# The embedding's products for four output tiles moved ahead, and the last gate product run as three tiles and one

## The chip, the core and the metric

The kernel runs on one core of one Trainium2 chip. The time is that of one execution on the device, in microseconds (us); "before" is the median of three runs. The engines are TensorE (PE, matmuls, with its weight loads as PEld), VectorE (DVE), ScalarE (ACT), GpSimd (POOL), and SyncE (SP), which here only issues DMA transfers.

## The reference, cut to what matters

One layer of a hybrid encoder block on 512 tokens of width 2048: two mixers, their gated merge, an output projection added to the residual, then a gated projection of the per-layer embedding `p` (256 wide), and a final RMSNorm:

```
merged = sigmoid(ga) * (a_out @ w_a_out) + sigmoid(gb) * (b_out @ w_b_out)
r = x + merged @ w_o
y = r + (p @ w_ple) * sigmoid(r @ w_ple_gate)
out = rmsnorm(y, final_gain)
```

## The kernel before, in words

Activations lie transposed, 128 channels by 512 tokens to a tile; 2048 channels are 16 tiles. Every product is made of float32 operands split in two parts of reduced type, high and low: high times high, high times low, low times high, that is three matmuls. ACT copies a tile to its high part and DVE subtracts it for the low part (line 136 and 141 for weights, 740 and 741 for activations, in `split`). Big products go in pairs of tiles through `gemm_pair` (line 264), seven products of half size each.

The order of every engine's instructions is the order in which the Python program emits them. `step()` is called after every third matmul or so; it runs functions that `later(n, f)` has put off by n steps, and takes one from the list `todo`. `split_to` and `load_to` split and load weights ahead of use (three and eight blocks ahead). Loads are issued by SP, in order.

SBUF tiles come from pools. `U(...)` gives one of `U_BUFS = 70` slots of 128x512 float32, `B(...)` one of 5 larger ones, raw weights one of 7. A tile holds its slot from the first instruction that touches it to the last one. Where no slot is free, the instruction that first writes the new tile waits for the last reader of a tile that gives one up, and its engine, in order, with it.

Towards the end of the program come these stages.

- `project_b`, 16 tiles of the second mixer's output projection, with the attention heads in between (ps_w, L196 to L198), then the first mixer's projection and the merge.
- the output projection in eight `gemm_pair` calls; in the last one `p_load` (L1165 to 1168) loads each half of the embedding from `pT` and splits it 22 steps later, and the parts of r that don't stay in SBUF are loaded again.
- the loop over 12 tiles of `p @ w_ple` (L1209 to 1230): six matmuls of 512 columns each into ps_pw, and ACT copies the result to a tile `pw`.
- six `gemm_pair` calls for 12 tiles of the gate, with `finish_y` behind them.
- the last four tiles (channels 1536 to 2047), in two pieces. For the first 384 tokens (slice `A`) `wide` (L1315 to 1335) goes over the 16 chunks k of r; for every k it makes three matmuls of 384 columns for each of the four tiles (ps_pg). Then ACT takes the sigmoid of all four; for each tile 6 matmuls give the embedding's product (ps_pw, L1332 to 1334), and DVE, POOL and ACT multiply, add to r, square, sum into `acc` and scale (L1346 to 1352). For the last 128 tokens (`C3`) `wide` is called again with tokens as rows ("natural"): 16 times three matmuls of 512 columns into ps_tg, then six for the embedding (ps_tw). Six steps into it `a_rms` has PE sum `acc` (ps_ms, L414), four steps later PE broadcasts the root (ps_bc, L425), and `a_out` scales and stores the 16 tiles (L1364).

While the natural piece runs, these U tiles are still to be read by it or behind it: 16 high and 16 low parts of r (`rh`, `rl`), the parts of ten weight blocks of 512 columns (20 tiles `wh4`, `wl4`: eight of the gate, two of the embedding), four parts of the embedding, `rn`, `fgn`, and 8 finished tiles (`pw`, of the first eight outputs). Before the natural piece, the four tiles `sg` of the gate's sigmoids are live as well.

Of the kernel before, what the change touches and what calls it, by code (L numbers as in the profile page):

```python
# [9 lines left out]
F32 = mybir.dt.float32  # L10
F32R = mybir.dt.float32r
# [23 lines left out]
def block_kernel(tc, xT, pT, posb, posq, w_in, w_v, w_ik, w_a, w_b, w_o, w_ple, w_gate,  # L35
# [4 lines left out]
    with contextlib.ExitStack() as ctx:  # L40
# [306 lines left out]
        u_p = [block(w_ple[:, 8 * q:8 * q + 8], (8,)) for q in range(MF // 4)]  # L347
# [759 lines left out]

        def project_b(m):
            gate_load(m + 2)
            pw = gemm(u_wb[m], bparts, "ps_w")  # L1110
            s = gates.popleft()
            dve.tensor_mul(s, pw, s)
            later(4, lambda: sp.dma_start(mbs[m], s))

        for m in range(16):
            project_b(m)
# [48 lines left out]
        def p_load(k):  # L1165
            t = U("pk")
            sp.dma_start(t, pT[:, k, :])
            later(22, lambda: pparts.append(split(t, "p", 1)))
# [40 lines left out]
        for m in range(MF):  # L1209
# [5 lines left out]
            ps = P("ps_pw")  # L1215
            for k in range(2):
                a, b = pparts[k]
                w = 2 * (m % 4) + k
                pe.matmul(ps, h[:, w], a, start=(k == 0), stop=False)
                pe.matmul(ps, h[:, w], b, start=False, stop=False)  # L1220
                pe.matmul(ps, l[:, w], a, start=False, stop=(k == 1))
                step()
# [6 lines left out]
            act.activation(t, ps, AF.Copy)  # L1229
            pws.append(t)  # L1230
# [4 lines left out]


        A, C3 = slice(0, 384), slice(384, 512)
# [98 lines left out]

        pgs = [P("ps_pg") for _ in range(4)]
        wide(u_t[0], rparts, pgs, range(4), False)
        sg = [U("sg") for _ in range(4)]
        for j in range(4):  # L1340
            act.activation(sg[j][:, A], pgs[j][:, A], AF.Sigmoid)
        for j in range(4):
            pw = P("ps_pw")
            wide(u_t[1], pparts, [pw], [j], False)
            y = ys[MF + j]
            dve.tensor_mul(sg[j][:, A], pw[:, A], sg[j][:, A])  # L1346
            (pool if j % 2 else dve).tensor_add(y[:, A], y[:, A], sg[j][:, A])
            act.activation(sg[j][:, A], y[:, A], AF.Square)
        for j in range(4):
            dve.tensor_add(acc[0][:, A], acc[0][:, A], sg[j][:, A])  # L1350
            y = ys[MF + j]
            act.activation(y[:, A], y[:, A], AF.Copy, scale=fg[:, MF + j:MF + j + 1])
# [177 lines left out]
```

## Time and profile before

| | |
|---|---|
| median of 3 runs | 1676.93 us (1675.07 to 1679.52) |
| the profiled execution | 1676.27 us, its span 1674.5 us |
| mean granted TensorE clock | 0.998 of full speed |
| PE busy | 1656.5 us, 99% |
| DVE, ACT, POOL busy | 1360.5, 927.8, 266.8 us |
| DMA | mean 228 GB/s, 381 MB |

The span goes from the first to the last instruction of the program; 1.8 us lie outside it. Busy matmuls overlap each other, so that the distance between starts is the cost of one. The rows of the trace stand below.

### The profile page before, as it was taken

How to read it: one execution, taken by the hardware profiler on the slowest of the kernel's cores; microseconds unless marked ns; L12 is line 12 of the kernel's file. 1: busy time of each engine (PE TensorE's matmuls, PEld its weight loads, DVE VectorE, ACT ScalarE, POOL GpSimd, SP SyncE). 2: the span in 40 equal slices, each digit the busy share in tenths (PEclk: the TensorE clock that was granted, in tenths of full speed). 3: DMA queues.
4: the chain of work that ended last, by engine and by line, in shares of the span. 5: the costliest groups of instructions: out<-in, count | busy, mean ns of one | idle time of the engine just before them, and what ended most of it. 6: DMA issues, size and time to landing. Idle time of an engine off the chain costs nothing.

```text
span 1674.5 us, 25823 instructions
## 1 busy us (share of the span) xinstructions
PE 1656.5 (99%) x9400; PEld 1446.7 (86%) x9400; DVE 1360.5 (81%) x2195; ACT 927.8 (55%) x1414; POOL 266.8 (16%) x266
## 2 busy tenths in 40 slices
PE   9999999999999999999999999999999999999997
PEld 7988888888888888888888888888888888888896
DVE  7898698988888888888888778676668888898895
ACT  7465455555555555455555545566643455477673
POOL 3100011111111111111331111100000243301202
PEclk9999999999999999999999999999999999999999
DMA  7536889788788788788998878999866699998873
GB/s 290 180 115 226 242 223 241 165 225 218 167 233 214 190 219 221 172 205 221 259 234 217 237 213 224 248 335 354 278 201 196 170 264 284 276 334 240 214 238 120
DMA packets 144608, 381.09 MB, mean 228 GB/s; under 512 B 15841, under 2 KB 32097, under 8 KB 144481
## 3 DMA queue, kind: packets, MB, share of 16 engines
q1 hardware_dynamic: 108416, 264.08, 45.8%
q0 software_dynamic: 26848, 98.58, 32.2%
q10 hardware_dynamic: 9216, 16.78, 2.8%
q8 instruction: 74, 1.21, 0.3%
q14 instruction: 54, 0.43, 0.1%
HBM read 326.82 MB, written 52.56 MB: 227 GB/s over the span
## 4 chain that ended last, share of the span: by engine, by line
PE 39%; DMA 8%; DVE 6%; ACT 2%; issue 1%; POOL 0%; SPq 0%; DVEq 0%; ACTq 0%
PE ps_p L264 13%; PE ps_v L264 8%; PE ps_r L264 4%; PE ps_q L264 4%; PE ps_w L196 2%; PE ps_w L197 2%; PE ps_w L198 2%; DVE wl L141 2%; DMA wraw<-w_o 1%; DMA mbs<-sg 1%; DMA sg<-sgb 1%; DVE e_t L234 1%; DMA wraw<-w_in 1%; ACT wh L136 1%; DMA bm<-scr 1%
## 5 line engine op out<-in xcount | busy, mean ns | idle before, releaser
L141 DVE TENSOR_TENSOR wl<-wraw,wh 128x1024 fp32r<-128x1024 f32 (+2 forms) x489 | 590.2, 1212 | 160.0 <-ACT wh L136 155.1
L136 ACT ACTIVATE wh<-wraw 128x1024 fp32r<-128x1024 f32 (+2 forms) x489 | 504.7, 1043 | 261.5 <-DVE wraw L143 125.3
L104 POOL DMA_DIRECT2D wraw<-w_in x132 | 116.8, 946 | 838.7 <-DVE wl L141 274.0
L230 ACT ACTIVATE e<-ps_p 128x512 f32<-128x512 f32 x174 | 103.8, 597 | 147.1 <-PE ps_p L264 138.0
L264 PE MATMUL ps_p<-hs,wh 128*128 128x512 f32 x704 | 177.0, 393 | 0.0
L264 PEld LDWEIGHTS ps_p<-hs,wh 128*128 128x128 f32 x704 | 126.5, 189 | 22.7
L264 PE MATMUL ps_p<-hs,wl 128*128 128x256 f32 x704 | 99.5, 283 | 0.8 <-DVE wl L141 0.8
L264 PEld LDWEIGHTS ps_p<-hs,wl 128*128 128x128 f32 x704 | 90.7, 191 | 2.1 <-DVE wl L141 1.2
L264 PE MATMUL ps_r<-hs,wh 128*128 128x512 f32 x352 | 90.4, 395 | 0.3 <-ACT wh L136 0.3
L264 PE MATMUL ps_p<-ha,wh 128*128 128x512 f32 x352 | 88.4, 392 | 0.0
L264 PE MATMUL ps_v<-ha,wh 128*128 128x512 f32 x352 | 88.2, 392 | 0.0
L264 PE MATMUL ps_q<-ha,wh 128*128 128x512 f32 x352 | 88.1, 392 | 0.0
L264 PE MATMUL ps_v<-hs,wh 128*128 128x512 f32 x352 | 86.9, 389 | 0.0
L915 DVE TENSOR_TENSOR go<-e_t 128x256 f32<-128x256 f32 x176 | 74.8, 425 | 6.2
L264 PEld LDWEIGHTS ps_v<-hs,wh 128*128 128x128 f32 x352 | 66.1, 188 | 13.8
L264 PEld LDWEIGHTS ps_v<-ha,wh 128*128 128x128 f32 x352 | 65.4, 188 | 13.5 <-issue 0.2
L264 PEld LDWEIGHTS ps_p<-ha,wh 128*128 128x128 f32 x352 | 63.2, 189 | 11.5 <-issue 0.3
L264 PEld LDWEIGHTS ps_q<-ha,wh 128*128 128x128 f32 x352 | 63.3, 189 | 11.3
L143 DVE TENSOR_TENSOR wraw<-wraw 128x1024 f32<-128x1024 f32 x58 | 71.0, 1225 | 2.0
L264 PEld LDWEIGHTS ps_r<-hs,wh 128*128 128x128 f32 x352 | 62.7, 189 | 11.3 <-ACT wh L136 0.5
L234 DVE TENSOR_TENSOR e_t<-ps_p,pv 128x512 f32<-128x512 f32 x52 | 35.8, 689 | 37.9 <-ACT e L230 37.8
L924 ACT ACTIVATE go<-go 128x512 f32<-128x512 f32 x40 | 25.3, 633 | 53.7 <-DVE go L915 53.7
(413 smaller groups left out, 3595.5 us busy)
## 6 DMA issues: line engine op xcount, KB each, us to landing
wraw<-w_in SPq DMA_DIRECT2D x190, 512.0 KB, 5.7
wraw<-w_in POOLq DMA_DIRECT2D x132, 512.0 KB, 8.4
wraw<-w_o SPq DMA_DIRECT2D x32, 512.0 KB, 8.1
wraw<-w_o POOLq DMA_DIRECT2D x24, 512.0 KB, 8.9
wraw<-w_gate SPq DMA_DIRECT2D x24, 512.0 KB, 5.4
wraw<-w_gate POOLq DMA_DIRECT2D x18, 512.0 KB, 6.6
wraw<-w_v SPq DMA_DIRECT2D x16, 512.0 KB, 4.6
wraw<-w_b SPq DMA_DIRECT2D x16, 512.0 KB, 6.9
```

Source lines behind the costliest of these rows:

```text
L104: pool.dma_start(out=raw_tiles[r], in_=src[:, k0:k0 + 8, :], accum_op=OP.add)
L136: act.activation(h, raw, AF.Copy)
L141: dve.tensor_sub(l, raw, h.bitcast(F32))
L143: dve.tensor_add(raw, raw, view(raw_tiles[plus], nk, cols))
L196: pe.matmul(o, h[:, k, w], a, start=(s == order[0]), stop=False)
L197: pe.matmul(o, h[:, k, w], b, start=False, stop=False)
L198: pe.matmul(o, l[:, k, w], a, start=False, stop=(s == order[-1]))
L230: act.activation(E[n], src, AF.Copy)
L234: f(t, x, y)
L264: pe.matmul(o[:, c], w[:, k], X[PRODUCTS[n]][k][:, c], start=(n < 4 and part == 0 and k == order[0]), stop=(part == parts[1] and k == orde ...
L915: dve.tensor_add(o[:, q], c0, c1)
L924: act.activation(o, o, func)
```

## The change

Four things are changed.

1. The embedding's halves are loaded and split once, in `project_b` before m = 9 and m = 12, stored as four tiles in DRAM (`ps_d`), and `p_load` loads the ready parts from there, both times it is called.
2. The loop of ps_pw goes over 16 tiles, the last four with 384 columns; a fourth block of `w_ple` is loaded and split for it. Their results are stored to DRAM (`pw_d`) and loaded again into four tiles `pw4` eight steps into the last gate stage.
3. In that stage `wide` is called for three tiles and then for the fourth; behind each call stand the sigmoid, product, sum, square and scaling of those tiles (`gated`). The 24 matmuls of ps_pw there are gone.
4. All sums of these tiles with r go to DVE; two of four were POOL's.

```diff
-        u_p = [block(w_ple[:, 8 * q:8 * q + 8], (8,)) for q in range(MF // 4)]
+        u_p = [block(w_ple[:, 8 * q:8 * q + 8], (8,)) for q in range(4)]
...
+        ps_d, pw_d = dp.tile([4, 128, L], F32, name="ps_d"), dp.tile([4, 128, L], F32, name="pw_d")
+
+        def p_split(k):
+            t = U("pk")
+            sp.dma_start(t, pT[:, k, :])
+
+            def both():
+                for i, part in enumerate(split(t, "p", 1)):
+                    later(8 + i, lambda i=i, part=part: sp.dma_start(ps_d[2 * k + i], part.bitcast(F32)))
+
+            later(12, both)
...
         for m in range(16):
+            if m in (9, 12):
+                p_split(m // 12)
             project_b(m)
...
         def p_load(k):
-            t = U("pk")
-            sp.dma_start(t, pT[:, k, :])
-            later(22, lambda: pparts.append(split(t, "p", 1)))
+            parts = U("ph", F32R), U("pl", F32R)
+            for i in range(2):
+                sp.dma_start(parts[i].bitcast(F32), ps_d[2 * k + i])
+            pparts.append(parts)
...
-        for m in range(MF):
+        A, C3 = slice(0, 384), slice(384, 512)
+        for m in range(16):
...
+            c = ALL if m < MF else A
             for k in range(2):
-                a, b = pparts[k]
+                a, b = pparts[k][0][:, c], pparts[k][1][:, c]
                 w = 2 * (m % 4) + k
-                pe.matmul(ps, h[:, w], a, start=(k == 0), stop=False)
+                pe.matmul(ps[:, c], h[:, w], a, start=(k == 0), stop=False)
...
-            act.activation(t, ps, AF.Copy)
-            pws.append(t)
+            act.activation(t[:, c], ps[:, c], AF.Copy)
+            if m < MF:
+                pws.append(t)
+            else:
+                later(6, lambda t=t, m=m: sp.dma_start(pw_d[m - MF, :, A], t[:, A]))
...
+        pw4 = [U("pw") for _ in range(4)]
+
+        def pw_loads():
+            for j in range(4):
+                sp.dma_start(pw4[j][:, A], pw_d[j, :, A])
+
+        later(8, pw_loads)
         pgs = [P("ps_pg") for _ in range(4)]
-        wide(u_t[0], rparts, pgs, range(4), False)
         sg = [U("sg") for _ in range(4)]
-        for j in range(4):
-            act.activation(sg[j][:, A], pgs[j][:, A], AF.Sigmoid)
-        for j in range(4):
-            pw = P("ps_pw")
-            wide(u_t[1], pparts, [pw], [j], False)
-            y = ys[MF + j]
-            dve.tensor_mul(sg[j][:, A], pw[:, A], sg[j][:, A])
-            (pool if j % 2 else dve).tensor_add(y[:, A], y[:, A], sg[j][:, A])
-            act.activation(sg[j][:, A], y[:, A], AF.Square)
-        for j in range(4):
-            dve.tensor_add(acc[0][:, A], acc[0][:, A], sg[j][:, A])
-            y = ys[MF + j]
-            act.activation(y[:, A], y[:, A], AF.Copy, scale=fg[:, MF + j:MF + j + 1])
+
+        def gated(js):
+            for j in js:
+                act.activation(sg[j][:, A], pgs[j][:, A], AF.Sigmoid)
+            for j in js:
+                y = ys[MF + j]
+                dve.tensor_mul(sg[j][:, A], pw4[j][:, A], sg[j][:, A])
+                dve.tensor_add(y[:, A], y[:, A], sg[j][:, A])
+                act.activation(sg[j][:, A], y[:, A], AF.Square)
+            for j in js:
+                dve.tensor_add(acc[0][:, A], acc[0][:, A], sg[j][:, A])
+                y = ys[MF + j]
+                act.activation(y[:, A], y[:, A], AF.Copy, scale=fg[:, MF + j:MF + j + 1])
+
+        for js in (range(3), range(3, 4)):
+            wide(u_t[0], rparts, [pgs[j] for j in js], js, False)
+            gated(js)
```

## Rows read from the trace of the kernel before

**Rows 1.** The page: busy us, share of the span, instructions.

```profile
PE 1656.5 (99%) x9400; PEld 1446.7 (86%) x9400; DVE 1360.5 (81%) x2195; ACT 927.8 (55%) x1414; POOL 266.8 (16%) x266
```

**Rows 2.** PE's waits over the span: us in total, times, longest.

```profile
PE ps_b L1395 <- POOL rl L1391: 3.7, 1, 3.7
...
PE ps_p L264 <- ACT wh L136: 1.6, 2, 1.3
...
PE ps_p L264 <- ACT e L230: 0.8, 1, 0.8
...
PE ps_mb L1303 <- DVE acc L1299: 0.2, 1, 0.2
```

**Rows 3.** Busy time by stretch: PE, PEld, DVE, ACT, POOL, clock, DMA share, GB/s.

```profile
1100.00:1200.00 100.00, 100.00 (x512) 85.48 (x511) 65.58 (x146) 65.34 (x143) 6.97 (x8) 1.00 1.01 337
...
1450.00:1500.00 50.00, 47.88 (x251) 40.99 (x250) 42.25 (x78) 33.30 (x66) 9.12 (x9) 1.00 1.01 319
...
1600.00:1625.00 25.00, 25.00 (x147) 23.68 (x146) 24.66 (x34) 17.43 (x28) 1.29 (x1) 1.00 0.69 238
```

**Rows 4.** PE in order of time, the last stages: start us, us.

```profile
1476.03 0.39 PE L1219 MATMUL ps_pw<-ph,wh 128*128 128x512 f32 x1
...
1496.58 2.11 PE L264 MATMUL ps_p<-ra,wh 128*128 128x512 f32 x8 [1.31 <-ACT wh L136]
...
1611.41 0.33 PE L1332 MATMUL ps_pg<-rh,wh 128*128 128x384 f32 x1
...
1645.87 0.33 PE L1332 MATMUL ps_pw<-ph,wh 128*128 128x384 f32 x1
...
1650.03 0.39 PE L1328 MATMUL ps_tg<-wh,rh 128*128 128x512 f32 x1
...
1654.16 0.72 PE L414 MATMUL ps_ms<-ones,acc 128*128 128x1 f32 x6
...
1663.52 0.39 PE L1330 MATMUL ps_tw<-wh,pl 128*128 128x512 f32 x1
```

**Rows 5.** ACT in order of time, around the loop of ps_pw.

```profile
1468.68 0.62 ACT L740 ACTIVATE ph<-pk 128x512 fp32r<-128x512 f32 x1
...
1495.47 1.06 ACT L136 ACTIVATE wh<-wraw 128x1024 fp32r<-128x1024 f32 x1
1496.41 1.09 ACT L1229 ACTIVATE y<-ps_pw 128x512 f32<-128x512 f32 x2
```

**Rows 6.** DVE in order of time, the last gate stage and behind it.

```profile
1618.40 1.22 DVE L141 TENSOR_TENSOR wl<-wraw,wh 128x1024 fp32r<-128x1024 f32 x1
...
1647.18 0.56 DVE L1346 TENSOR_TENSOR sg<-ps_pw,sg 128x384 f32<-128x384 f32 x1 [7.46 <-PE ps_pw L1334]
1647.77 0.56 DVE L1347 TENSOR_TENSOR y<-y,sg 128x384 f32<-128x384 f32 x1
1648.25 0.55 DVE L1346 TENSOR_TENSOR sg<-ps_pw,sg 128x384 f32<-128x384 f32 x1
...
1650.80 3.17 DVE L1350 TENSOR_TENSOR acc<-acc,sg 128x384 f32<-128x384 f32 x4
...
1664.10 0.41 DVE L1384 TENSOR_TENSOR sg<-ps_tw,sg 128x256 f32<-128x256 f32 x1
```

**Rows 7.** ACT in order of time, the last gate stage.

```profile
1644.57 1.99 ACT L1341 ACTIVATE sg<-ps_pg 128x384 f32<-128x384 f32 x4 [5.57 <-PE ps_pg L1334]
1648.37 0.53 ACT L1348 ACTIVATE sg<-y 128x384 f32<-128x384 f32 x1 [1.80 <-DVE y L1347]
...
1652.69 2.12 ACT L1352 ACTIVATE y<-y,g_sb 128x384 f32<-128x384 f32 x4
```

**Rows 8.** SP's waits from 1590 to 1640 us.

```profile
SPq L1268 <- DVE y L1245: 4.1, 1, 4.1
```

**Rows 9.** The stretches around PE's last idle time (columns as in rows 3).

```profile
1667.00:1668.00 1.00, 0.43 (x3) 0.43 (x4) 0.10 (x1) 0.45 (x1) 0.51 (x1) 1.00 1.03 361
1668.00:1669.00 1.00, 0.28 (x3) 0.09 (x1) 0.69 (x4) 0.44 (x2) 0.49 (x2) 0.77 1.04 372
1669.00:1670.00 1.00, 0.00 (x0) 0.00 (x0) 1.00 (x6) 0.00 (x0) 0.80 (x2) 0.50 1.03 352
```

**Rows 10.** PE's first matmuls of the program.

```profile
1.26 4.45 PE L401 MATMUL ps_warm<-warm 128*128 128x512 bf16 x10 [1.26 <-DVE warm L396]
```

More of the change, by code (lines that the diff above doesn't have):

```diff
@@ L1215, in block_kernel @@
             ps = P("ps_pw")
+            c = ALL if m < MF else A
             for k in range(2):
-                a, b = pparts[k]
+                a, b = pparts[k][0][:, c], pparts[k][1][:, c]
                 w = 2 * (m % 4) + k
-                pe.matmul(ps, h[:, w], a, start=(k == 0), stop=False)
-                pe.matmul(ps, h[:, w], b, start=False, stop=False)
-                pe.matmul(ps, l[:, w], a, start=False, stop=(k == 1))
+                pe.matmul(ps[:, c], h[:, w], a, start=(k == 0), stop=False)
+                pe.matmul(ps[:, c], h[:, w], b, start=False, stop=False)
+                pe.matmul(ps[:, c], l[:, w], a, start=False, stop=(k == 1))
                 step()
@@ L1228, in block_kernel @@
                 t = ypair[m // 2][:, L * (m % 2):L * (m % 2) + L]
-            act.activation(t, ps, AF.Copy)
-            pws.append(t)
+            act.activation(t[:, c], ps[:, c], AF.Copy)
[3 more added lines that the diff above has]
+                later(6, lambda t=t, m=m: sp.dma_start(pw_d[m - MF, :, A], t[:, A]))
         ys = {}
-        A, C3 = slice(0, 384), slice(384, 512)
         def finish_y(m, s, r):
```

## The prediction

> **What bounds the kernel now.** I read the page first: PE is busy 99% of the span [rows 1]. So a change wins only where PE waits or in the end behind PE's last matmul, and a matmul that is moved costs the same elsewhere. PE's waits are few [rows 2]. The longest, 3.7 us, lies in the end; of the others 0.8 us (on ACT's copy of `e`) and 1.3 of the 1.6 us (on ACT's `wh`) frame the loop that the change lengthens. The stretch from 1450 to 1500 us shows those two as 2.12 us of PE idle, at a DMA share of 1.01 [rows 3]. The order of time gives the last stages [rows 4]: the gate stage starts at 1611.41, its 24 matmuls of ps_pw take 1645.87 to 1650.03 (4.16 us, 0.173 each), the natural piece starts at 1650.03, PE sums `acc` at 1654.16, and its last matmul starts at 1663.52. In between PE never pauses, but DVE is nearly as full in the gate stage, 24.66 of 25 us [rows 3]. The end hangs on two things that finish together: PE's ps_tw, and DVE's scaling of the tiles, behind which the tail's first product starts at 1664.10 [rows 6].
>
> **Part 1, the matmuls.** The 24 leave the gate stage and come into the ps_pw loop, with as many columns: 4.16 us less, 4.16 us more, 0 in sum.
>
> **Part 2, around the loop.** ACT and DVE lose the embedding's splits there (two of 0.62 us on ACT [rows 5]), which now lie in `project_b`, where PE waits for nothing at 66% DVE and 65% ACT [rows 3]; there they cost nothing, and if that cover is gone, their 1.2 us. ACT's copy of `e`, 0.81 us late, comes 1.2 us earlier, so that pause should vanish. PE's pause of 1.31 us at 1496.58 [rows 4] comes from a `wh` that starts at 1495.47 behind queued copies of ps_pw [rows 5]. In the new loop PE needs it 4.2 us later, while ACT in front of it gets one more block of `w_ple` (1.06) and the four copies that came after it (2 x 1.1), 3.3 us, less the 1.2 for the splits. So most of this pause goes as well. I take -1.5 us for both. Bounds: -2.1 (both gone) and +1.5. The upper bound is for DMA: this stretch gains 512 KB of weights, 512 KB in `p_load`, and 768 KB of stores, 1.8 MB, 5.6 us at its 319 GB/s [rows 3], against 4.2 us of PE time. The 1.5 MB more in `project_b` come near 1173 and 1196 us, beside a busy DMA (share 1.01) but loads that are eight blocks ahead: I take 0.
>
> **Part 3, three tiles and one.** With four tiles PE spends 12 matmuls on a chunk k, 2.08 us; with three, 9, 1.56 us. It eats weights and parts of r by a third faster, and DVE, full, makes them in the same order as before. Chunk 4 needs a low part that is ready at 1618.40 + 1.22 = 1619.62 [rows 6], 8.2 us behind the start of the stage. Before, PE wanted it 8.33 + 0.35 = 8.7 us behind the start; now at 6.24 + 0.35 = 6.6. That is a wait of 1.7 us on DVE, which was none. From there DVE's order shifts in favour of the weights, and the remaining chunks keep pace within half a microsecond by my count, with SP's queue (four loads of `pw4` and four parts of the embedding instead of two halves, in front of the later gate weights) the most doubtful. I take +2.2; bounds 0 (DVE starts the stage earlier) and +4 (loads late).
>
> **Part 4, the slots.** The price here is not a duration but a count. A new tile waits for a slot's last reader: in the trace SP waits 4.1 us for DVE's L1245 before a load into a tile of the B pool, whose slot the last gate tile gives up there [rows 8]. In the U pool, at the end of the three tiles' pass, live are 8 `pw`, 32 parts of r, 20 parts of weights, 4 of the embedding, `rn` and `fgn`: 66. Before, the four `sg` made it 70, exactly the pool. Now `pw4` holds four from early in the stage, so 70 are taken before any `sg`. The first U tile to be freed is the high part of r's first tile, after the second matmul of the natural piece. So the sigmoids that should run under the fourth tile's pass wait until that pass is over. Nothing on PE waits for them until `acc` is summed; on ACT everything queues behind the first sigmoid.
>
> Counted from the start of the natural piece (T): the second matmul is through at 0.63 (starts 0.23 apart: 18 matmuls in 4.13 us [rows 4]). ACT starts 0.1 us later; sigmoids follow at 0.48 (four in 1.99 [rows 7]). DVE does product and sum at 0.59 and 0.48 from start to start [rows 6], on DVE alone since POOL is dropped: product 0 at 1.29, sum 2 over at 4.58, squares by 5.15 (0.53 each), third `acc` sum over at 6.24. Behind the squares ACT's queue holds three scalings (0.53 each [rows 7]) to 6.7, then the fourth sigmoid to 7.2; product, sum, square and `acc` of tile 3 add 2.3: about 9.55, and PE starts its sum at 9.7. Before it did at 4.13 (`acc` was ready at 1650.80 + 3.17 = 1653.97, just in time [rows 6]). PE therefore stands 5.6 us inside the natural piece, with ten steps of it and all of `a_out` behind. Those keep their distances, so the end moves by 5.6. Bounds: 0 (a slot is free after all) and 6.5.
>
> **Part 5, the clock.** After PE's last long matmul (over at 1663.91) the granted clock is still 1.00 in 1667 to 1668, falls in the next microsecond (0.77), and is 0.50, 1.2 GHz, after it [rows 9]: some 4.6 us, with only small matmuls in between. A pause of 5.4 us is longer, so I let the clock fall. For the way back the nearest row is the start: ten matmuls of 512 columns take 4.45 us [rows 10], 0.445 each against 0.229 later, though the profile's clock column there shows no fall. Half speed over 4.5 us costs 2.2. Bounds 0 and 4.
>
> The Trainium skill (TensorE: Matmul & The Clock Gate, part 1 on the clock gate) says that the throttled state is the default and that activity lifts it. By it the matmuls behind the pause would start at half rate and the sum is the one below; by a clock that holds through one pause, it is 2.2 us less. The trace agrees with its two levels, but has no long pause in mid-program.
>
> **Sum.** -1.5 + 2.2 + 5.6 + 2.2 = 8.5; on the profiled execution's 1676.27 us that is 1684.8. The median of the runs lies 0.7 above that execution, so I predict 1685 us.
>
> **The rivals.** A change under 0.3% (5.0 us) is about what a measurement here can't tell from none: "same" is 1671.9 to 1682.0.
>
> - *The sigmoids are not held* (0.33). If one U slot is free at the end of the pass, three tiles' gating runs under the fourth's 8.3 us, and the fourth's 2.9 us fit in front of PE's sum. Then the sum is -1.5 + 2.2: 1677, not slower. For it speaks that the change splits the stage so that this can run; against it the count, exact to one slot. It decides at one slot.
> - *Held, but the clock stays up* (0.20): 1682.6 to 1683. The fall was seen once, after 4.6 us, against a pause of 5.4.
> - *DMA becomes the bound* (0.08). The 1.8 MB at share 1.01 arrive late at the first gate products and the new loads delay the gate weights; with +1.5 and +4 in parts 2 and 3 the sum is 1676.3 + 1.5 + 4 + 5.6 + 2.2 = 1690. Against it: from 1500 us on PE waits for no load.
> - *Faster by over 5 us* (0.05). Both pauses around the loop are 2.1 us and nothing else is shortened: behind ps_tw stands the same tail. I see no mechanism that gives 5.
>
> **How the numbers follow.** The forecast with the clock's fall has 0.34, its own range 1683 to 1688. The range of 1675.5 to 1689 takes in the two rivals next to it and leaves out most of the last two and the edge of the first. Slower: 0.34, 0.14 of the 0.20, and 0.08, 0.56 in all. Same: 0.33 and 0.06, 0.39. Faster: 0.05.
>
> **What would show it.** In the new profile: PE's sum of `acc` (ps_ms) some 9.7 us behind the first ps_tg, with a wait on DVE of over 5 us; the first sigmoid of `sg` behind the first ps_tg and not behind the third tile's ps_pg; a PE wait on `wl` of about 1.7 us in the fifth chunk of the three tiles' pass; the 0.8 and 1.3 us around the ps_pw loop gone; a granted clock under 1.00 in the natural piece. The prediction is wrong if the sigmoids start during the fourth tile's pass, or if PE waits in front of the gate products for weights.

## The result, and the profile after

The changed kernel takes 1698.17 us (median of 4 runs, 1696.57 to 1698.77) against 1676.00 for the kernel before on the same chip: a ratio of 1.0129, 95% interval 1.0117 to 1.0140. The prediction had the sign and missed the size: 1685 us, range 1675.5 to 1689. The profiled execution of the changed kernel takes 1698.77 us, its span is 1697.0, 22.5 more than before.

TensorE's waits over the whole span (us in total, times, longest) are the first view to lay beside [rows 2]:

```profile
PE ps_ms L414 <- DVE acc L1373: 5.0, 1, 5.0
PE ps_v L264 <- ACT wh L136: 4.3, 1, 4.3
PE ps_b L1422 <- POOL rl L1418: 3.7, 1, 3.7
PE ps_p L264 <- DVE wl L141: 3.4, 6, 1.3
PE ps_pg L1351 <- DVE wl L141: 1.7, 2, 1.5
PE ps_pg L1349 <- ACT wh L136: 1.5, 1, 1.5
...
PE ps_pt L1025 <- ACT bm L1016: 0.8, 3, 0.3
...
PE ps_pg L1351 <- DVE whl L141: 0.5, 1, 0.5
```

The 3.7 us at the end are the old ones. The 0.8 us on `e` are gone, as forecast. The first line and the `wl` line of ps_pg are the two waits that the prediction names. The second line, 4.3 us on a copy `wh` in front of ps_v, is a wait for weights in front of the gate products; the prediction has no term for it and names such a wait as a sign of being wrong. TensorE in order of time shows where they lie; it answers to [rows 4]:

```profile
1477.34 0.39 PE L1236 MATMUL ps_pw<-ph,wh 128*128 128x512 f32 x1
...
1498.21 0.98 PE L264 MATMUL ps_v<-rs,wh 128*128 128x512 f32 x3
...
1510.98 1.22 PE L264 MATMUL ps_p<-rs,wl 128*128 128x256 f32 x8 [1.32 <-DVE wl L141]
...
1513.88 1.98 PE L264 MATMUL ps_v<-ra,wh 128*128 128x512 f32 x8
1515.69 1.11 PE L264 MATMUL ps_v<-ra,wl 128*128 128x256 f32 x8
...
1523.89 3.78 PE L264 MATMUL ps_v<-rs,wh 128*128 128x512 f32 x8 [4.29 <-ACT wh L136]
1527.47 1.91 PE L264 MATMUL ps_v<-rs,wl 128*128 128x256 f32 x8
...
1624.25 0.33 PE L1349 MATMUL ps_pg<-rh,wh 128*128 128x384 f32 x1
...
1632.52 0.44 PE L1351 MATMUL ps_pg<-rh,wl 128*128 128x384 f32 x1 [1.49 <-DVE wl L141]
...
1645.61 0.45 PE L1349 MATMUL ps_pg<-rh,wh 128*128 128x384 f32 x1 [1.48 <-ACT wh L136]
...
1663.95 0.39 PE L1345 MATMUL ps_tg<-wh,rh 128*128 128x512 f32 x1
...
1673.25 1.44 PE L414 MATMUL ps_ms<-ones,acc 128*128 128x1 f32 x6 [5.01 <-DVE acc L1373]
...
1679.81 0.89 PE L425 MATMUL ps_bc<-cs,ra 128*128 128x128 f32 x6
...
1685.78 0.39 PE L1347 MATMUL ps_tw<-wh,pl 128*128 128x512 f32 x1
```

Read from one landmark to the next, the 22.5 us split without remainder. "Gate pairs" is the stretch from the first ps_v on `rs` behind the loop (1492.35 before, 1498.21 now) to the first ps_pg; "gate stage" from there to the first ps_tg.

| stretch | before, us | now, us | more by | forecast |
|---|---|---|---|---|
| start to attention (first ps_w on `bh`) | 1102.95 | 1103.39 | 0.44 | 0 |
| attention with `project_b` | 126.00 | 127.69 | 1.69 | 0 |
| to the first ps_pw | 247.08 | 246.26 | -0.82 | part of -1.5 (the pause on `e`) |
| ps_pw loop | 16.32 | 20.87 | 4.55 | 4.16 |
| gate pairs | 119.06 | 126.04 | 6.98 | the rest of -1.5 |
| gate stage | 38.62 | 39.70 | 1.08 | -4.16 + 2.2 |
| first ps_tg to ps_ms | 4.13 | 9.30 | 5.17 | 5.6 |
| ps_ms to ps_bc | 3.43 | 6.56 | 3.13 | 2.2 |
| ps_bc to the end of the span | 16.91 | 17.19 | 0.28 | 0 |

Busy time by stretch confirms the three rows in question. The columns are those of [rows 3]; first the kernel before (attention, gate pairs, gate stage), then the changed one:

```profile
1102.95:1228.95 126.00, 125.88 (x641) 107.12 (x640) 78.64 (x173) 79.44 (x179) 6.10 (x7) 1.00 0.90 297
1492.35:1611.41 119.06, 117.75 (x674) 103.50 (x672) 102.31 (x135) 84.88 (x123) 22.56 (x21) 1.00 0.87 245
1611.41:1650.03 38.62, 38.38 (x223) 38.06 (x222) 27.29 (x44) 20.60 (x38) 2.30 (x2) 1.00 0.41 130
```

```profile
1103.39:1231.08 127.69, 126.70 (x641) 107.11 (x640) 79.79 (x175) 80.44 (x181) 6.83 (x8) 1.00 0.91 305
1498.21:1624.25 126.04, 120.43 (x674) 105.50 (x673) 100.07 (x127) 82.92 (x117) 22.91 (x21) 0.97 0.84 235
1624.25:1663.95 39.70, 35.79 (x199) 33.67 (x198) 23.63 (x37) 16.98 (x30) 1.76 (x1) 1.00 0.48 160
```

In the attention the work is the same 641 matmuls; the two more entries of DVE and ACT are the embedding's splits, and TensorE's idle time grows from 0.12 to 0.99 us. In the gate pairs idle time grows from 1.31 to 5.61 us and the granted clock falls to 0.97 in the mean.

**The late weight copy.** The chain behind the 4.29 us runs through three engines. SyncE's queue, GpSimd and ScalarE of the changed kernel in order of time:

```profile
1500.96 0.32 SPq L1250 DMA_DIRECT2D pw_d<-pw  x1
1501.33 0.93 SPq L115 DMA_DIRECT2D wraw<-w_gate  x1
```

```profile
1513.35 0.86 POOL L104 DMA_DIRECT2D wraw<-w_gate  x1 [10.25 <-issue]
```

```profile
1522.79 2.00 ACT L136 ACTIVATE wh<-wraw 128x1024 fp32r<-128x1024 f32 x2 [7.47 <-DMA wraw<-w_gate]
...
1644.41 0.63 ACT L740 ACTIVATE rh<-y 128x512 fp32r<-128x512 f32 x1 [4.46 <-DMA y<-rr]
...
1664.62 1.25 ACT L1366 ACTIVATE sg<-ps_pg 128x384 f32<-128x384 f32 x3 [11.32 <-PE ps_tg L1346]
```

The second gate pair's raw weights are loaded from 1501.33 and land 11.4 us later; GpSimd then starts the transfer that adds a second block to them (the sum, for short) at 1513.35, and ScalarE copies the sum to its high part at 1522.79, when that has landed too. Counted from the first gate matmul: load at +3.1, sum started at +15.1, copy at +24.6. In the kernel before, the same load and sum (the second of the two sums in the grouped line, 1498.19 + 1.77 - 0.88 = 1499.08) are

```profile
1491.93 0.42 SPq L115 DMA_DIRECT2D wraw<-w_gate  x1
```

```profile
1498.19 1.77 POOL L104 DMA_DIRECT2D wraw<-w_gate  x2 [5.36 <-DVE wl L141]
```

that is load at -0.4, sum at +6.7, and the copy at +18.5 (1510.81). So the load starts 3.5 us later against TensorE and takes 11.4 us to land instead of 5.3. From the load to the start of the sum it is 12.0 us instead of at most 7.2, from there to the copy 9.4 instead of 11.7; in all the copy is 6.1 us later.

**The clock.** The stretches around the two long pauses (columns as in [rows 3], to be read beside [rows 9]):

```profile
1522.00:1524.00 2.00, 0.10 (x1) 0.11 (x1) 0.12 (x1) 1.21 (x2) 0.00 (x0) 0.73 0.06 25
1524.00:1526.00 2.00, 2.00 (x5) 1.61 (x6) 1.97 (x3) 1.98 (x2) 0.49 (x1) 0.50 0.00 0
...
1672.00:1673.00 1.00, 0.00 (x0) 0.00 (x0) 0.41 (x2) 0.89 (x2) 0.00 (x0) 1.00 0.00 0
1673.00:1674.00 1.00, 0.75 (x4) 0.76 (x4) 0.19 (x1) 0.25 (x1) 0.00 (x0) 0.55 0.00 0
1674.00:1675.00 1.00, 1.00 (x5) 1.00 (x5) 0.16 (x1) 0.00 (x0) 0.04 (x1) 0.50 0.00 0
...
1679.00:1680.00 1.00, 1.00 (x5) 0.81 (x4) 0.00 (x0) 0.00 (x0) 0.00 (x0) 0.53 0.00 0
```

After both pauses the granted clock is 0.50, the 1.2 GHz level. Behind the first, eight matmuls of ps_v on `wh` and eight on `wl` take 3.78 and 1.91 us; ps_v on `ra` further up takes 1.98 and 1.11 for as many, so this pause costs 2.6 us more than its length. Pause, clock and the 1.32 us at 1510.98, less the 1.31 us that stood there before [rows 4], make 6.9 of the 6.98 us of the gate pairs.

### The profile page after: what moved, and what is told of

Same layout as the page of the kernel before. It is cut to its first block, busy times and chain, and to the rows that moved or that the text cites. A ratio compares the mean times of both kernels' runs of the same rounds, so it can differ in the third digit from the quotient of the medians.

```text
span 1697.0 us, 25857 instructions
## 1 busy us (share of the span) xinstructions
PE 1665.6 (98%) x9400; PEld 1450.7 (85%) x9400; DVE 1361.7 (80%) x2196; ACT 928.5 (55%) x1417; POOL 264.7 (16%) x264
## 4 chain that ended last, share of the span: by engine, by line
PE 35%; DMA 9%; DVE 6%; ACT 4%; issue 2%; POOL 0%; SPq 0%; DVEq 0%; ACTq 0%; POOLq 0%
PE ps_p L264 12%; PE ps_v L264 8%; PE ps_r L264 4%; PE ps_q L264 4%; DMA wraw<-w_o 2%; PE ps_w L197 2%; PE ps_w L196 2%; PE ps_w L198 2%; DVE wl L141 2%; ACT wh L136 1%; DMA mbs<-sg 1%; DMA wraw<-w_gate 1%; DMA wraw<-w_in 1%; DVE e_t L234 1%; DMA bm<-mnd 1%
## 5 line engine op out<-in xcount | busy, mean ns | idle before, releaser
L264 PEld LDWEIGHTS ps_p<-ha,wh 128*128 128x128 f32 x352 | 63.2, 189 | 11.6 <-issue 0.3
L264 PEld LDWEIGHTS ps_r<-hs,wh 128*128 128x128 f32 x352 | 62.7, 189 | 11.6 <-ACT wh L136 0.7
```

The costliest lines, as they stand in the source:

```text
L264: pe.matmul(o[:, c], w[:, k], X[PRODUCTS[n]][k][:, c], start=(n < 4 and part == 0 and k == order[0]), stop=(part == parts[1] and k == orde ...
```

## The experiments

All times are medians, with the ratio to the kernel before in the same series and its 95% interval; its medians there were 1676.0 to 1677.5 us. The last three columns, in us, are read from the one profiled execution of each kernel: the length of the gate pairs, the start of the second gate pair's weight sum on GpSimd behind the first gate matmul, and TensorE's wait of ps_v on `wh`.

| kernel | median, us (runs) | ratio | gate pairs | sum at | wait |
|---|---|---|---|---|---|
| before | 1676.00 (4) | 1 | 119.06 | 6.7 | 0 |
| changed | 1698.17 (4) | 1.0129 [1.0117, 1.0140] | 126.04 | 15.1 | 4.3 |
| e1_slots | 1688.27 (5) | 1.0062 [1.0042, 1.0083] | 124.45 | 14.2 | 5.0 |
| e2_stores_act | 1696.11 (4) | 1.0105 [1.0083, 1.0126] | 126.53 | 16.5 | 5.5 |
| e4_three_one | 1678.75 (10) | 1.0005 [0.9995, 1.0015] | 119.60 | 9.5 | 0 |
| e5_split_once | 1680.95 (10) | 1.0017 [1.0004, 1.0030] | 124.18 | 14.8 | 3.1 |
| e7_moved | 1685.26 (4) | 1.0052 [1.0039, 1.0066] | 119.29 | 9.9 | 0 |
| e8_no_trip | 1687.56 (4) | 1.0060 [1.0038, 1.0082] | 122.28 | 9.1 | 0 |
| e9_half | 1677.86 (11) | 1.0008 [1.0000, 1.0017] | 119.99 | 10.8 | 0 |
| e10_no_bytes | 1686.04 (4) | 1.0054 [1.0037, 1.0072] | 123.64 | 10.2 | 0 |
| e11_half_trip | 1688.52 (4) | 1.0065 [1.0051, 1.0079] | 125.92 | 15.7 | 5.3 |
| e12_loads_act | 1682.09 (8) | 1.0033 [1.0021, 1.0044] | 121.09 | 12.1 | 0.4 |
| e13_pw_pool | 1686.21 (4) | 1.0061 [1.0044, 1.0078] | 124.76 | 14.9 | 5.4 |
| e14_less_x | 1687.56 (4) | 1.0056 [1.0039, 1.0073] | 126.66 | 15.9 | 6.0 |
| e15_before_less_x | 1674.09 (10) | 0.9983 [0.9973, 0.9992] | 118.81 | 8.2 | 0 |
| e16_less_r | 1683.47 (4) | 1.0042 [1.0027, 1.0057] | 119.60 | 10.5 | 0.3 |
| e17_three_blocks | 1684.90 (4) | 1.0051 [1.0033, 1.0070] | 120.80 | 11.6 | 1.5 |
| e18_before_less_r | 1676.95 (10) | 0.9997 [0.9987, 1.0007] | 118.83 | 6.7 | 0 |
| e19_mended | 1686.75 (4) | 1.0052 [1.0036, 1.0068] | 126.19 | 16.2 | 5.7 |

### The parts one by one

**e1_slots**: the changed kernel without the four `sg` tiles. The sigmoid is written over its PSUM operand, product and square over `pw4`.

```diff
-                act.activation(sg[j][:, A], pgs[j][:, A], AF.Sigmoid)
+                act.activation(pgs[j][:, A], pgs[j][:, A], AF.Sigmoid)
...
-                dve.tensor_mul(sg[j][:, A], pw4[j][:, A], sg[j][:, A])
+                dve.tensor_mul(pw4[j][:, A], pw4[j][:, A], pgs[j][:, A])
```

> The changed kernel, with the sigmoids of the last four tiles written back into their PSUM banks and the products and squares into the tiles pw4, so that no tile sg is wanted while the U pool is full; arithmetic, loads and stores unchanged. Theory (the slots held the sigmoids back): the first sigmoid starts behind the third tile's matmuls, PE's wait of 5.0 us in front of ps_ms and the slow clock behind it (3.1 us) go; about 1690 us against 1698. Rival (the gating of three and one is late by itself, or the clock falls anyway): the wait stays above 3 us and the time above 1695.

9.9 us less than the changed kernel (the medians are of different series). ps_ms stands 4.12 us behind the first ps_tg instead of 9.30, ps_bc 3.41 behind ps_ms instead of 6.56: those are the two distances of the kernel before (4.13 and 3.43), 8.3 us together. The sigmoids now run under the fourth tile's pass:

```profile
1652.68 1.51 ACT L1364 ACTIVATE ps_pg<-ps_pg 128x384 f32<-128x384 f32 x3 [1.49 <-PE ps_pg L1351]
```

that is 9.2 us ahead of the first ps_tg, where they started 0.7 behind it. So it is shown that the missing slots held them back, and that the slow clock goes when the pause goes. The count, exact to one slot, isn't tested: the edit spares four. It leaves 0.6% over the kernel before.

**e2_stores_act**: the changed kernel, with the products stored by ScalarE's queue.

```diff
-                later(6, lambda t=t, m=m: sp.dma_start(pw_d[m - MF, :, A], t[:, A]))
+                later(6, lambda t=t, m=m: act.dma_start(pw_d[m - MF, :, A], t[:, A]))
```

> The changed kernel, with the four stores to pw_d issued by ACT instead of SP; the same bytes. Theory (the stores stand in SP's queue in front of the gate weights and wait there for ACT's late copies): the weights of the second gate pair are issued 1 to 4 us earlier, PE's wait of 4.3 us in front of ps_v at 1524 and the slow clock behind it (2.7 us) mostly go; about 1692 us. Rival (the transfers themselves are too many for a busy DMA): the wait stays and the time is within 1.5 us of 1698.

2 us less (the intervals of the two ratios overlap), and the wait stays, at 5.5 us. The load goes out at +4.1, not earlier than +3.1. That the stores stand in front of the gate weights on SyncE's queue is not what makes them late; this theory fell.

**e4_three_one**: the kernel before, with nothing but the last gating as three tiles and one (its products stay in the gate stage).

```diff
...
+        for js in (range(3), range(3, 4)):
+            wide(u_t[0], rparts, [pgs[j] for j in js], js, False)
+            gated(js)
```

> The kernel before, with only the last gate stage changed to three tiles and one; the embedding's products stay there, 18 matmuls behind the three tiles and 6 behind the fourth. Theory (the pace of three tiles alone outruns DVE): a PE wait of about 1.7 us on wl in the fifth chunk and some more, 1678 to 1680 us. Rival (only the new loads in SP's queue make the weights late): no wait in that pass and 1676, the time before.

The two waits of ps_pg on `wl` (1.5) and `whl` (0.5) appear here by themselves, and the gate stage takes 40.70 us instead of 38.62, 2.08 more. In the time of the whole it is hardly to be told from nothing.

**e5_split_once**: the kernel before, with nothing but the embedding split once by way of DRAM (`p_split` in `project_b`, four loads in `p_load`).

```diff
...
+            if m in (9, 12):
+                p_split(m // 12)
             project_b(m)
...
-            t = U("pk")
-            sp.dma_start(t, pT[:, k, :])
-            later(22, lambda: pparts.append(split(t, "p", 1)))
+            parts = U("ph", F32R), U("pl", F32R)
+            for i in range(2):
+                sp.dma_start(parts[i].bitcast(F32), ps_d[2 * k + i])
+            pparts.append(parts)
```

> The kernel before, with only the embedding split once, stored to DRAM and loaded as parts. Theory (the splits moved into the attention heads' stretch disturb it by about a microsecond, and the pause of 0.8 us on ACT's copy of e goes): 1675.5 to 1677 us, with PE waits on the attention's bm of about 0.8 us. Rival (these disturbances come from elsewhere in the changed kernel, and both pauses around the ps_pw loop shrink): 1674 us.

Slower by 0.17%, with runs from 1676.26 to 1682.88. The attention takes 127.71 us; it takes 127.66 to 127.73 in the thirteen traces with `p_split` and 126.00 to 126.07 in the six without. In its profiled execution, the longest of its runs, the gate pairs have the wait on `wh` that the changed kernel has, without any moved product.

**e7_moved** and **e8_no_trip**: the kernel before, with nothing but the products moved (sigmoids in place, four gated at once, all their sums on DVE); the second leaves out the stores and loads of `pw_d`, the gate multiplies `y` by the sigmoid instead.

```diff
-                later(6, lambda t=t, m=m: sp.dma_start(pw_d[m - MF, :, A], t[:, A]))
+                pass
...
-                dve.tensor_mul(pw4[j][:, A], pw4[j][:, A], pgs[j][:, A])
+                dve.tensor_mul(pw4[j][:, A], y[:, A], pgs[j][:, A])
```

> The kernel before with the second part of the change alone: the sixteen-turn loop and the round trip of the four products through DRAM (0.79 MB out, 0.79 MB back), gating four at once, sigmoids in place, the embedding split twice as before. Bytes theory (the stretch from 1440 to 1512 us moves data at the limit of the 16 DMA engines, so each further megabyte puts off the gate weights by about 3.3 us at 300 GB/s): the four stores cost up to 2.6 us, so 1678 to 1681 us, with a TensorE wait of ps_v on ACT wh of 1 to 3 us near 1520. Order theory (the gate weights stand one w_ple block further back, so that their copy has less lead over TensorE): the same time, but then e8 keeps it. Third possibility (only the embedding's four loads do it): 1677 to 1678, no such wait.

> As e7_moved without the round trip: the four products are computed and copied, but not stored nor loaded, and the gate multiplies y itself in their place (the output of the last four tiles is not the reference's). Bytes theory: the wait of ps_v on ACT wh is gone or under 1 us, 1676.5 to 1678.5 us, at least 1.5 us less than e7_moved. Order theory: within 1 us of e7_moved, the wait stays.

Both theories miss. Moving alone costs 9 us, more than either gave it, and without a wait of ps_v on `wh`. By its landmarks e7_moved is 9.9 us over the span of before: 3.7 lie ahead of the attention, where the two kernels are the same, and stay unexplained; the loop takes 4.7 more and the gate stage only 2.6 less, and behind it come 1.9 for `acc` and 1.7 for a slow clock. e8_no_trip gets its 4.6 us back in the gate stage (33.98), so the loads of the last stage are what e7_moved and the changed kernel lack there; but it loses them again in front, with pauses on `wl` of 3.2 us in the gate pairs and of 3.9 in all ahead of the loop (1.3 there in the kernel before), the latter in instructions that the two kernels share.

**e9_half** and **e10_no_bytes**: two loads of the embedding's parts instead of four; the low part is the high one again. The first on e5_split_once, the second on e1_slots, there without the round trip too.

```diff
-            parts = U("ph", F32R), U("pl", F32R)
-            for i in range(2):
-                sp.dma_start(parts[i].bitcast(F32), ps_d[2 * k + i])
-            pparts.append(parts)
+            h = U("ph", F32R)
+            sp.dma_start(h.bitcast(F32), ps_d[2 * k])
+            pparts.append((h, h))
```

> As e5_split_once, but only the high half of the embedding is loaded back (two loads of 256 KB as in the kernel before, not four), and it stands for the low half too (products not the reference's). Bytes theory: the 3.5 us by which e5_split_once was slower come from the second half megabyte (1.7 us at 300 GB/s) and what it pushes back: 1677 to 1679 us. Order theory (the split in the attention and the shifted slots do it): 1680 to 1682 us, as e5_split_once.

> As e1_slots (the whole change with the sigmoids in place) without the round trip and with half of the embedding's loads, so that it moves no more bytes between 1440 and 1512 us than the kernel before (output not the reference's). Bytes theory: 1688.3 falls by 5 to 7 us, to 1681 to 1683 us; what is left is the three-and-one gating (1.3) and the split's 1 us in the attention. Order theory: 1686 to 1689 us, and the TensorE wait of ps_v on ACT wh stays at 4 to 5 us.

e9_half does what the bytes theory says. In e10_no_bytes the sum comes early as well (10.2), but another weight is late: two loads of `w_gate` now go out at +0.8 and +1.3, and a sum of the first pair, started at +1.1 between them, is ready 4.4 us after ScalarE wanted it. The time falls by less than expected. e8_no_trip shows the same (4.0 us).

**e11_half_trip**, **e12_loads_act**, **e13_pw_pool**: e1_slots with e9's edit; e5_split_once with the four loads on ScalarE's queue; e1_slots with the loads of `pw4` on GpSimd's. The edits of the second and third:

```diff
-                sp.dma_start(parts[i].bitcast(F32), ps_d[2 * k + i])
+                act.dma_start(parts[i].bitcast(F32), ps_d[2 * k + i])
...
-                sp.dma_start(pw4[j][:, A], pw_d[j, :, A])
+                pool.dma_start(pw4[j][:, A], pw_d[j, :, A])
```

> As e1_slots, but with only the high half of the embedding loaded back (two loads of 256 KB, not four, in front of the gate pairs and again in the last stage); the products' round trip stays (output not the reference's). In the ten traces so far the fourth weight sum of GpSimd after the loop stands 14.2 to 16.5 us behind the first gate matmul in the four kernels with four loads, and 6.7 to 10.8 us in the six with two. Load theory: it comes at about 10 us here, the wait of ps_v on ACT wh (5.0 in e1_slots) is under 1 us, the gate pairs take 119 to 121 us instead of 124.5, and the time is 1683 to 1685 us. Rival (the round trip's stores, or the place of the gate weights one block later, make that wait): 1687 to 1690 us, the wait stays above 3 us.

> As e5_split_once with the four loads of the embedding's halves started by ScalarE's queue instead of SyncE's: the same bytes at nearly the same time, but nothing of it ahead of other loads on SyncE. Load theory by bytes (the half megabyte more takes 1.7 us of a stretch at the limit): the fourth weight sum still 13 us or more behind the first gate matmul, 1680 to 1683 us. Rival (it is the order on SyncE's queue): the sum at 6.7 to 10.8 us, the wait of ps_v on ACT wh gone, 1677 to 1679.5 us.

> As e1_slots with the four loads of the products in the last stage started by GpSimd's queue instead of SyncE's, where they stand ahead of the y<-rr and embedding loads. If that order makes ScalarE's weight copies late there, the TensorE waits of ps_pg on ACT wh (0.7) go and the gate stage takes 38 us instead of 39.1: 1687 us. If it is the bytes, nothing changes: 1688 us. In both cases the wait of ps_v on ACT wh (5.0) stays.

e11_half_trip goes against the load theory: with half a megabyte less the sum is at 15.7 and the wait at 5.3. In e12_loads_act the time is the theory's, the wait is the rival's (0.4), and the sum at 12.1 is neither's. Neither a single load nor a single queue makes this wait. e13_pw_pool settles another point: the wait of ps_pg on `wh` is gone and the gate stage takes 37.21 us instead of 39.10. The changed kernel's 1.48 us there come from SyncE's order in the last stage, the loads of `pw4` ahead of `y<-rr`. In its median, over four scattered runs, this doesn't show against e1_slots.

### Which stretch is full

**e14_less_x** and its control **e15_before_less_x**: of the loads of `x` in the down-projection every second is left out (2 MB between 1316 and 1460 us), and the sum adds its other operand twice.

```diff
-                sp.dma_start(xc[i], xT[:, m + 8 * i, :])
+                if i == 0:
+                    sp.dma_start(xc[i], xT[:, m + 8 * i, :])
...
-                e.tensor_add(xc[i][:, q], xc[i][:, q], c0)
+                e.tensor_add(xc[i][:, q], c0 if i else xc[i][:, q], c0)
```

> As e1_slots, but the eight loads of the second half of x between 1316 and 1460 us are left out (2 MB), the sum there adds the down-projection's result to itself instead, with the same instructions (output not the reference's). Nothing of the change's own lines differs. Theory: the 16 DMA engines are busy at a share of 0.95 to 1.05 from 1356 to 1517 us, so that every byte put into that stretch, whichever it is, moves the gate weights; 2 MB less at about 280 GB/s give back some 7 us of DMA time, more than the 6 us by which the weight copy came late, so that the wait of ps_v on ACT wh (5.0 in e1_slots) is gone, the gate pairs take 118 to 121 us instead of 124.5, and the time is 1682 to 1684.5 us. Rival (the place of the gate weights in the order of the work, or the engines' queues): the wait stays above 3 us, 1687 to 1690 us.

> The kernel before with the same 2 MB left out (output not the reference's): the control. Theory: its weight copies there were hardly late (TensorE waits of 1.3 and 0.8 us), so 1675 to 1677 us, at most 2 us faster. If it falls by as much as e14_less_x does against e1_slots, the missing bytes say nothing about the change.

The theory of one limit from 1356 us on fell: the wait is 6.0 us. The DMA share is 1.00 from 1360 to 1440 us without these bytes too, at 277 to 281 GB/s, where the same engines carry 367 later. The stretch from the attention's end to the first ps_pw gets shorter by 3.9 us against e1_slots and by 2.7 in the control against before, and the control as a whole is 0.17% faster; in e14_less_x the weights behind that stretch land no sooner against TensorE.

**e16_less_r** and its control **e18_before_less_r**: eight of the twenty kept operand tiles of the gate products, loaded between 1467 and 1500 us, are not loaded, and their neighbours stand for them. Also 2 MB, but just ahead of the late copy.

```diff
+            if n not in RAW and k % 2:
+                Xr[n][k] = Xr[n][k - 1]
+                return
             Xr[n][k] = t = U("r" + n, F32R)
```

**e17_three_blocks**: the moved products use the third block of `w_ple` again, so that the fourth is neither loaded nor split.

```diff
-        u_p = [block(w_ple[:, 8 * q:8 * q + 8], (8,)) for q in range(4)]
+        u_p = [block(w_ple[:, 8 * q:8 * q + 8], (8,)) for q in range(MF // 4)]
...
-            i = u_p[m // 4][0]
-            if m % 4 == 0:
+            i = u_p[min(m // 4, 2)][0]
+            if m % 4 == 0 and m < MF:
```

> As e1_slots, but of the twenty kept operand tiles of the gate products that are loaded back from 1467 to 1500 us (256 KB each) eight are not loaded; their neighbours stand for them (output not the reference's). That takes 2 MB out of just the 40 us ahead of the late weight copy and leaves the order of the weight blocks as it is. Local theory (the DMA engines are at their limit from about 1465 to 1515 us, and the gate weights wait behind these tiles): the fourth weight sum comes at 10 us or less behind the first gate matmul instead of 14.2, the wait of ps_v on ACT wh (5.0) is under 1 us, gate pairs 119 to 121 us, 1682 to 1684.5 us. Rival (one more block of w_ple in the ring of seven raw weight buffers puts the second gate pair's load back): the wait stays above 3 us, 1687 to 1690 us.

> As e1_slots, but the four moved products take the third block of w_ple again, so that the fourth is neither loaded nor split (output not the reference's): the ring of raw weight buffers stands as in the kernel before, and 0.5 MB less is moved. Ring theory: the second gate pair's load is issued about 4 us earlier against the gate matmuls (at -0.4 us as before, not +3.1), and the wait of ps_v on ACT wh (5.0) is gone: 1682 to 1684 us. Local theory (bytes alone): 0.5 MB of 2 are gone, the wait falls to 3 to 4 us, 1686 to 1688 us.

> The kernel before without the eight loads that e16_less_r leaves out (output not the reference's): the control for it. If those 2 MB count only where the change has filled the stretch, it stays within 2 us of the kernel before (1675 to 1677.5 us), against the 4.8 us by which e16_less_r beat e1_slots; if they are worth the same here, e16_less_r says nothing about the change.

Here the wait goes, as the local theory said. SyncE's load and GpSimd's sum of the second gate pair, and the DMA share in the ten microseconds on either side of the first gate matmul (columns as in [rows 3]), in e1_slots:

```profile
1501.41 0.71 SPq L115 DMA_DIRECT2D wraw<-w_gate  x1
```

```profile
1512.52 0.86 POOL L104 DMA_DIRECT2D wraw<-w_gate  x1 [9.34 <-issue]
```

```profile
1488.29:1498.29 10.00, 9.95 (x50) 8.50 (x48) 8.31 (x21) 9.14 (x23) 0.00 (x0) 1.00 1.04 367
1498.29:1508.29 10.00, 10.00 (x56) 8.71 (x56) 6.16 (x9) 9.28 (x18) 1.76 (x2) 1.00 1.04 269
```

and in e16_less_r:

```profile
1501.94 0.60 SPq L115 DMA_DIRECT2D wraw<-w_gate  x1
```

```profile
1509.30 0.86 POOL L104 DMA_DIRECT2D wraw<-w_gate  x1 [5.60 <-issue]
```

```profile
1488.81:1498.81 10.00, 9.94 (x50) 8.51 (x48) 8.33 (x21) 9.14 (x23) 0.00 (x0) 1.00 0.91 331
1498.81:1508.81 10.00, 10.00 (x56) 8.71 (x56) 6.92 (x10) 9.21 (x18) 1.76 (x2) 1.00 0.76 172
```

The load goes out at the same +3.1 us in both. In e1_slots it lands after 10.5 us and it is 11.1 until the sum starts; in e16_less_r that is 6.7 and 7.4, and TensorE's wait is

```profile
PE ps_v L264 <- ACT wh L136: 0.3, 1, 0.3
```

instead of 5.0. In the changed kernel and in e1, e2, e11, e13, e14 and e19, which all keep these eight loads, it is 4.3 to 6.0 (e10_no_bytes, whose load goes out at +0.8, has none). The gate pairs come back to 119.60 us, and the ratio falls from 1.0062 to 1.0042 (3.4 us, with intervals that overlap; the medians, of different series, differ by 4.8), while the control does not move (0.9997). e17_three_blocks lies between and fits neither theory's numbers: sum at 11.6, wait 1.5 where 0.5 MB of bytes alone were to leave 3 to 4. Its load still goes out at +3.1, so the ring of raw buffers is not what holds it.

That the DMA engines are full there is not what the change brought. The kernel before has as high a share there (columns: TensorE, clock, DMA share, GB/s), and its load lands after 5.3 us:

```profile
1482.35:1492.35 10.00, 10.00 (x46) 1.00 1.05 396
1492.35:1502.35 10.00, 8.69 (x49) 1.00 1.04 324
```

So has e7_moved ahead of its first gate matmul; its load also goes out at +3.1, and it lands after 6.1 us:

```profile
1490.38:1500.38 10.00, 9.77 (x48) 1.00 1.04 374
```

What differs is when SyncE sent the five loads of r in front of it, first in e1_slots, then in e7_moved:

```profile
1497.68 2.72 SPq L1170 DMA_DIRECT2D rs<-rq  x5
```

```profile
1497.24 2.93 SPq L1158 DMA_DIRECT2D rs<-rq  x5
```

They go out from -0.6 to +2.1 us in e1_slots and from -3.1 to -0.2 in e7_moved; in e16_less_r only three are left, out by -3.4. That these five make the load late is a reading of the traces; no run moves them alone.

**e19_mended**: the whole change, with sigmoids in place, the embedding's loads on ScalarE's queue and those of `pw4` on GpSimd's (the edits of e1_slots, e12_loads_act and e13_pw_pool together).

> The whole change, computing the reference's output, with what the runs found taken out: sigmoids in place in PSUM, the embedding's loads on ScalarE's queue and the products' loads of the last stage on GpSimd's. Theory: as e1_slots (1688.3) less up to 4 us at the gate pairs and 1 to 2 in the gate stage, 1683 to 1686 us; the kernel before is not beaten, since the loop's 4.6 us come back in the gate stage with 4.2 at most, and the split costs 1.7 us in the attention and the three-and-one gating 2. Rival: the bytes are the same, so the weight copy stays late and the time is that of e1_slots, 1687 to 1690 us.

The gate stage takes 36.51 us, but the wait of ps_v on `wh` is there with 5.7 us: the rival's mechanism, at a time between the two. The bytes are what they were. This agrees with the Trainium skill (DMA: Bandwidth & Descriptors, Issuing engines are not separate DMA queues), by which transfers started from several engines run on the same 16 DMA engines and only the time to start them is saved; e2_stores_act with its 5.5 us agrees too, e12_loads_act (0.4 us) only in part. No version of the change in this table beats the kernel before.

## Why the prediction missed

**Part 1 held.** The loop grew by 4.55 us, 0.4 more than counted, about half of that in one late start inside it (ps_pw at 1495.98 stands 0.39 us behind the matmul before, not 0.17); without the loads of the last stage the gate stage gives 4.64 back (e8_no_trip).

**Part 2 is the step that failed**, in two places, and by 10 of the 14 us that are missing: 1.7 in the attention, where it had 0, and 6.6 around the loop and in the gate pairs (-0.82 + 0.4 + 6.98), where it had -1.5. Of the rest, 3.0 us are part 3's and 0.9 part 5's.

First, "there they cost nothing" of the splits in `project_b`. They cost about 1.7 us in every trace that has them, above even the 1.2 named for lost cover. The 66% and 65% of [rows 3] are a mean over a stretch with chains inside it: with two ScalarE copies and two DVE subtractions more, TensorE waits three times for ScalarE's `bm` of the softmax (0.8 us in all) and once for DVE's `mx` (0.2), and from start to start these four pauses cost 1.7. Which of the added instructions or transfers delays them, no run separates.

Second, the DMA bound. It set 5.6 us of transfers against 4.2 us of added TensorE time and kept 1.5 as the worst that could come. Both pauses around the loop did go, as taken, though one of 1.32 us came in their place at 1510.98. But what counted for the next stage was not the sum of the bytes, it was when one transfer landed: the second gate pair's weights start 3.5 us later against TensorE, take 6.1 us longer to land, and the copy of their sum is 6.1 us late. The kernel before has no TensorE wait for a load behind 1500 us, and I took this for slack; the copy came at +18.5 there, already 1.34 us after ScalarE wanted it. The pause then drew the half clock after it, 2.6 us that no term had.

So the rival to which I gave 0.08, that DMA becomes the bound, came true, beside the forecast and not in its place. Its 1690 is 8 short mostly for the same two reasons: nothing for the attention, and 1.5 for a pause that costs 4.3 + 2.6.

**Part 3** was right in its mechanism and too small. The wait on DVE's `wl` was forecast at 1.7 us (8.2 - 6.6 of its own figures is 1.6) and is 1.49, and the two waits of e4_three_one cost 2.08 with their restarts, against 2.2. "The remaining chunks keep pace" failed at the point that was called most doubtful: SyncE's queue. ScalarE waits 4.46 us for `y<-rr`, TensorE 1.48, and e13_pw_pool takes that away. In all 5.24 us (39.70 - 38.62 + 4.16), above the bound of 4.

**Part 4 held.** The first sigmoid starts at 1664.62, behind the second matmul of the natural piece, as counted, and not in the fourth tile's pass; ps_ms follows the first ps_tg by 9.30 us against 9.7, 5.17 later than before against 5.6.

**Part 5** had the right mechanism and a term too small: 3.13 us instead of 2.2. The granted clock was at or near 0.50 for over 6 us (still 0.53 in 1679 to 1680), not 4.5 as taken from [rows 10].

**What stays open.** That transfers just ahead of the gate pairs make the load late is shown by e16_less_r with its control. How the change puts them in its way in each case isn't: e7_moved with the loop and the stores but the old loads escapes, e5_split_once with the new loads alone does not always, and e11_half_trip with half of them does not. All are one profiled execution each, in a stretch where a load that comes two microseconds later meets other transfers. Nor is it settled why e7_moved costs 9 us when its stages account for about 6.

## What to carry to other kernels

Where DMA stands at a share of 1, as it did here before the change too, don't price added transfers as bytes over rate against time: look up the next load that an engine waits for, how long it takes from issue to landing there, and how much lead its consumer has left; a small wait in the trace of before means that the lead is used up. A share of busy time over a whole stage says nothing about a chain inside it that sets the pace; look for that chain before calling an engine free. And count buffers: the slots that four more long-lived tiles take were worth 8 us here, and writing in place gave them back.

## What the runs showed of the hardware

A pause of TensorE can cost more than its length. Behind 4.3 us the granted clock was 0.50 for about 5 us; in e5_split_once, behind a pause of 3.1 us, it was 0.56 and 0.58 in the two stretches of 2 us from 1518 to 1522. The length alone doesn't tell: e7_moved and e8_no_trip have the same pause of 1.7 us in front of ps_ms, the first ran at 0.50 from 1663 to 1666 us and took 5.13 us to ps_bc, the second stayed at 1.00 and took 3.52.

A DMA share of 1.00 can hide very different rates: 277 to 281 GB/s in the down-projection, where 2 MB less did nothing for the wait behind it, and 367 GB/s at a share of 1.04 ahead of the gate pairs, where 2 MB less took a wait of 5.0 us down to 0.3. Nor does the share tell whether a load is late: ahead of the gate pairs it is 1.05 (396 GB/s) in the kernel before and 1.04 (372 GB/s) in the changed one, and the load lands after 5.3 us in the one and 11.4 in the other.
